# Turning from layer 0 to layer 1 in a two-layer encoder step: order of ScalarE and Pool, two more PSUM banks for the output sums, three early value tiles

## The chip, the cores and the metric

The kernel runs on one core of one Trainium2 chip. The metric is device time in microseconds of one execution, start to end. Of the core's engines the text names PE (TensorE, the matmuls), ACT (ScalarE), DVE (VectorE), POOL (GpSimd) and SP (SyncE, which issues most transfers). Every engine works through its own list of instructions in order; an instruction that waits holds up all behind it on that engine.

## The reference

One step of a two-layer encoder for 512 prompt rows and 64 sample rows of width 1024, in float32. Each layer normalises, projects, mixes in two attention branches, projects out, normalises again and adds. What matters for the change is the seam between the layers: layer 0's `rmsnorm(mp, norm_post)` and sum, layer 1's `rmsnorm(xp, norm_pre)`, and the first q, k and v of layer 1's band attention.

```python
def rmsnorm(x, g):
    y = x * lax.rsqrt(jnp.mean(x * x, axis=-1, keepdims=True) + EPS)
    return y * g

for l in range(DEPTH):
    hp, hs = rmsnorm(xp, norm_pre[l]), rmsnorm(xs, norm_pre[l])
    if l % 2 == 0:
        mp, stp = even_mixer(hp, pos_p, None, *w)
        ms, sts = even_mixer(hs, pos_s, caches, *w)
    else:
        mp, stp = odd_mixer(hp, pos_p, None, *w)
        ms, sts = odd_mixer(hs, pos_s, caches, *w)
    xp = xp + rmsnorm(mp, norm_post[l])
    xs = xs + rmsnorm(ms, norm_post[l])

# in odd_mixer: q_c, k_c, v_c, ... = split_cols(h @ w_in, ODD_SIZES)
# return mixed @ w_out, states
```

## The kernel before

The 512 prompt rows are four tiles of 128, called t0 to t3; the 64 sample rows are a fifth tile, NT (the number 4). Float32 products are made of three matmuls on a high and a low part of each factor: ACT casts the high part (L173 for weights, L224 for activations), and POOL (L177, weights) or DVE (L225, activations) subtracts to get the low part. PSUM has eight banks, dealt out in rings: psA 2, psS 2, psT 2, psU 1, psX 1 (L119).

**The end of layer 0** is `out_second` (L718). For each tile, in the order NT, t0 to t3, it makes four sums of 256 columns (c = 0 to 3, 12 matmuls each for a prompt tile, L270), in a bank of psA. DVE adds the bank to the partial result `m` (L745). After every second sum ACT squares the half row (L747) with the sum of squares read out behind it, into the bank of psX. After the fourth, POOL makes the root in two steps, `rstd_of2` (L197, L198); `m` is multiplied by the norm's weights (L751, on POOL for NT, t0, t1, on DVE for t2 and t3), and DVE multiplies by the root and adds the residual (L754). Then `sink0` (L1200) writes the row out, takes the next norm, `put_h` (L205: two squares on ACT L211, root on POOL, product on DVE L214), and `put_hT` (L217) transposes the result in eight 128x128 transposes on PE (L221) into psT; ACT copies the high part (L224), DVE makes the low part (L225). `out_second` runs again at the end of layer 1, with a sink that only writes the rows out (L1398).

**The start of layer 1** clears some tiles on POOL (L1221, L330, L334, L335), prepares bias tiles there (L1232, L1233, L1271) and starts the first pair of band heads, `qk_pair` (L337). Its q and k are made in two cuts of the rows (L35): the first takes rows 0 to 255 (t0, t1; 24 + 24 matmuls of 256 columns, L260), the second rows 256 to 575 (t2, t3, NT; 24 + 24 matmuls of 320 columns). `q_cb` empties a q bank (ACT L347, DVE L348, once for each of the two heads), `k_cb` a k bank (ACT L364 twice and L365, POOL L371, a transfer). Between the cuts, `early_v` makes value tiles t0 and t1 (24 matmuls each, L270, then a copy on ACT L407, a split on DVE, a transfer out). Behind the second cut and the transposes of k (L382, L384) come value tiles t2, t3 and NT (L278 is the sample's).

The order of each engine's list is not written by hand: a scheduler orders all instructions when the program is built, by its own estimate of when each would be ready, within the dependences and the priorities in the text (`tc.high_priority`). So an edit that moves one instruction can move others. `tc.issue_after(x)` keeps the instructions inside it behind x where both are on the same engine; it adds no wait between engines.

## Time and profile before

| | |
|---|---|
| time, median of 3 runs (lowest, highest) | 835.13 us (834.76, 836.82) |
| the profiled execution's own time | 829.8 us |
| its span, first to last instruction | 827.9 us |
| granted PE clock, mean | 0.984 of full speed |
| busy: PE, DVE, ACT, POOL | 93%, 61%, 60%, 46% of the span |
| the turn, layer 0's last sums to layer 1's sample value tile | about 380 to 455 us |

All times in the text are microseconds from the start of the profiled span. In a timeline row the first number is the start, the second the length, then engine, line, operation, output<-input, shape and count, and in brackets how long the engine was idle before and whose end released it. A matmul's length is that of the pipeline; the next starts before it ends, so the pace is read from the starts.

### The profile page before, as it was taken

What the parts mean: (1) busy time and instruction counts of PE and PEld (TensorE: products, weight loads), DVE (VectorE), ACT (ScalarE), POOL (GpSimd) and SP (SyncE); (2) the same over time, 40 slices, a digit from 0 to 9 for tenths busy, and PEclk for the clock granted to TensorE, in tenths of its full rate; (3) what the DMA queues carried; (4) which work ended last, traced back from release to release, by engine and by line L of the source; (5) the groups of instructions that cost most, each with busy time, mean ns of one, the idle gap of its engine ahead of it and who ended that gap; (6) DMA issues with size and microseconds to landing.
All of it is one profiled execution on the core that took longest, in us unless ns stands there. A gap on an engine that the chain in (4) does not pass through costs nothing.

```text
span 827.9 us, 16285 instructions
## 1 busy us (share of the span) xinstructions
PE 766.3 (93%) x5581; PEld 713.1 (86%) x5581; DVE 507.6 (61%) x1318; ACT 499.2 (60%) x1342; POOL 382.6 (46%) x461
## 2 busy tenths in 40 slices
PE   6989999999997999989868999999997999999986
PEld 4989899989895888788767999999897899998986
DVE  4544765777847675738962654664754576658345
ACT  7554664776747675666542755575644767768521
POOL 7584342654427131055772644553344444546453
PEclk9999999999999999999998999999999999999999
DMA  8243324441123022146352443433223543551562
GB/s 271 60 145 114 101 73 146 142 122 53 54 68 109 29 73 74 40 139 218 122 171 72 123 118 104 136 110 99 87 81 111 170 127 111 158 140 55 158 228 102
DMA packets 69924, 95.52 MB, mean 115 GB/s; under 512 B 9529, under 2 KB 40489, under 8 KB 69810
## 3 DMA queue, kind: packets, MB, share of 16 engines
q1 hardware_dynamic: 69264, 94.12, 37.7%
q8 instruction: 44, 0.72, 0.4%
q14 instruction: 38, 0.31, 0.2%
q10 hardware_dynamic: 578, 0.37, 0.1%
HBM read 74.36 MB, written 18.79 MB: 113 GB/s over the span
## 4 chain that ended last, share of the span: by engine, by line
PE 70%; DVE 10%; ACT 7%; DMA 5%; issue 4%; POOL 4%; SPq 1%; DVEq 0%; POOLq 0%; ACTq 0%
PE psA L260 27%; PE psA L270 15%; PE psU L435 5%; PE psX L528 4%; PE psT L426 4%; PE psA L278 3%; PE psS L563 2%; PE psS L460 2%; PE psS L461 2%; POOL m L751 1%; DMA part<-part 1%; PE psT L509 1%; ACT whi L173 1%; DMA x<-in_x_prompt_dram 1%; PE psA L989 1%
## 5 line engine op out<-in xcount | busy, mean ns | idle before, releaser
L260 PE MATMUL psA<-hT,whi 128*128 128x320 f32 (+1 forms) x1216 | 258.5, 301 | 3.8 <-DVE foxqbl L353 2.0
L177 POOL TENSOR_TENSOR wlo<-wraw,whi 128x512 fp32r<-128x512 f32 (+2 forms) x130 | 168.6, 1307 | 188.4 <-ACT whi L173 146.2
L260 PEld LDWEIGHTS psA<-hT,whi 128*128 128x128 f32 x1216 | 198.8, 190 | 6.8 <-issue 2.7
L260 PE MATMUL psA<-hT,wlo 128*128 128x320 f32 (+1 forms) x608 | 183.5, 302 | 0.0
L270 PE MATMUL psA<-whi,hT 128*128 128x256 f32 (+2 forms) x812 | 162.8, 287 | 6.8 <-DVE m L745 5.5
L270 PEld LDWEIGHTS psA<-whi,hT 128*128 128x128 f32 x812 | 130.0, 188 | 9.5 <-DVE m L745 6.4
L270 PE MATMUL psA<-wlo,hT 128*128 128x256 f32 (+2 forms) x420 | 121.2, 288 | 0.0
L260 PEld LDWEIGHTS psA<-hT,wlo 128*128 128x128 f32 x608 | 115.8, 190 | 0.8
L173 ACT CAST whi<-wraw 128x512 fp32r<-128x512 f32 (+2 forms) x130 | 78.2, 616 | 39.8 <-PE psA L260 21.4
L270 PEld LDWEIGHTS psA<-wlo,hT 128*128 128x128 f32 x420 | 79.5, 189 | 0.8
L371 POOL TENSOR_TENSOR kz<-kf,r 64x256 fp32r<-64x256 f32 x48 | 36.7, 765 | 30.5 <-ACT kf L365 28.8
L430 DVE TENSOR_TENSOR pt1l<-psT,pt1h 128x384 fp32r<-128x384 f32 x64 | 39.6, 620 | 14.6 <-ACT pt1h L429 13.7
L1237 DVE CUSTOM_DVE_ANT_0 x<-psS,T 128x128 f32<-128x128 f32 (+1 forms) x64 | 31.0, 484 | 23.0 <-PE psT L426 8.5
L447 POOL TENSOR_TENSOR g<-g,oT 128x512 f32<-128x512 f32 x14 | 18.3, 1304 | 53.8 <-DVE oT L439 53.5
L541 POOL TENSOR_TENSOR sK<-kraw,sK 128x384 fp32r<-128x384 f32 (+2 forms) x32 | 30.3, 946 | 26.3 <-ACT sK L540 24.6
L469 ACT ACTIVATE psS<-x,st 128x128 f32<-128x128 f32 (+1 forms) x64 | 34.1, 532 | 13.8 <-DVE st L1237 13.5
L429 ACT CAST pt1h<-psT 128x384 fp32r<-128x384 f32 x64 | 33.9, 531 | 12.6 <-PE psT L426 11.7
L528 PE MATMUL psX<-vs,sP 128*128 128x256 f32 (+1 forms) x184 | 38.6, 303 | 1.5 <-DVE sP L515 1.2
L439 DVE SCALAR_TENSOR_TENSOR oT<-psU,oT 64x256 f32<-64x256 f32 x64 | 26.8, 419 | 18.6 <-ACT oT L438 17.7
L460 PE MATMUL psS<-r,r 128*128 128x256 f32 (+1 forms) x96 | 35.4, 370 | 2.6 <-DVE st L1237 1.7
L347 ACT ACTIVATE r<-psA 64x256 fp32r<-64x256 f32 x48 | 18.2, 378 | 32.4 <-PE psA L260 16.9
L472 DVE TENSOR_SCALAR x<-psS,st 128x128 f32<-128x128 f32 (+1 forms) x64 | 35.1, 548 | 1.3
(390 smaller groups left out, 1893.9 us busy)
## 6 DMA issues: line engine op xcount, KB each, us to landing
wraw<-in_ws_dram SPq DMA_DIRECT2D x80, 256.0 KB
wraw<-in_w_out_dram SPq DMA_DIRECT2D x32, 256.0 KB
x<-in_x_prompt_dram SPq DMA_DIRECT2D x16, 256.0 KB
part<-part SPq DMA_DIRECT2D x32, 128.0 KB
m<-part SPq DMA_DIRECT2D x16, 256.0 KB
r<-r SPq DMA_DIRECT2D x48, 64.0 KB
out_dram<-kout SPq DMA_DIRECT2D x12, 256.0 KB
out_dram<-vf SPq DMA_DIRECT2D x24, 128.0 KB
```

The source lines that it names most:

```text
L173: nc.scalar.copy(hi, raw)
L177: eng.tensor_sub(lo, raw, f32(hi))
L260: nc.tensor.matmul(ps[:, :c1 - c0], w[:, k % 4, :], h.m[k // 4][:, k % 4, x, c0:c1], start=(k == 0 and n == 0), stop=(k == KT - 1 and n == 2))
L270: nc.tensor.matmul(ps[:, :n], h.m[k // 4][:, k % 4, x, t * P:(t + 1) * P], w[:, k % kp, :], start=(k == ks[0] and m == 0), stop=(k == ks[- ...
L371: nc.gpsimd.tensor_sub(pair.kl[s][me, cs], kf[me, cs], f32(k[me, cs]))
L429: nc.scalar.copy(ph[:, :i + 1, at], tv)
L430: nc.vector.tensor_sub(pl[:, :i + 1, at], tv, f32(ph[:, :i + 1, at]))
L435: nc.tensor.matmul(po, m.v[p // 2, j][:, p % 2, s * P:(s + 1) * P], x[:, j, :], start=(j == 0 and x is ph), stop=(j == 2 * hq + 1 and x is ...
L460: nc.tensor.matmul(ps[:, :w], pair.qq[s][:, q], pair.kk[s][:, :w], start=True, stop=False)
L469: nc.scalar.activation(ps[:, :n], src, AF.Exp, bias=mn, scale=-1.0, accum_out=sm)
L472: nc.vector.tensor_scalar(out=w[:, :n], in0=ps[:, :n], scalar1=rs, scalar2=None, op0=ALU.mult)
L528: nc.tensor.matmul(po[:, :256], l, r, start=(first and n == 0), stop=(last and n == len(ops) - 1))
```

## The change

Four edits. (1) The ACT instructions that empty the banks of the first cut (`q_cb`, `k_cb`) are kept behind the last square of layer 0's `out_second`. (2) The clearing and bias work on POOL is kept behind the last root, that of t3's `put_h`. (3) In `out_second` the odd sums (c = 1, 3) of t1 to t3 go to the banks of psS instead of psA, in both layers. (4) `early_v` makes three value tiles, t0, t1 and t2.

```diff
--- before.py
+++ after.py
@@ -1,4 +1,4 @@
-from contextlib import ExitStack
+from contextlib import ExitStack, nullcontext
 
 import numpy as np
 
@@ -195,8 +195,10 @@
 
         v, r = St([P, 1]), St([P, 1])
         RS.tensor_scalar(out=v[:rows], in0=ss[:rows, :1], scalar1=ss[:rows, 1:], scalar2=EPS, op0=ALU.add, op1=ALU.add)
-        nc.gpsimd.tensor_tensor(out=r[:rows], in0=v[:rows], in1=mhalf[:rows], op=ALU.pow)
+        roots.append(nc.gpsimd.tensor_tensor(out=r[:rows], in0=v[:rows], in1=mhalf[:rows], op=ALU.pow))
         return r
+
+    roots = []
 
     RS = nc.gpsimd if RSP else nc.vector
     ROOT = 1.0 / 32
@@ -334,13 +336,24 @@
         nc.gpsimd.memset(f32(m.qbh), 0.0)
         nc.gpsimd.memset(f32(m.qbl), 0.0)
 
-    def qk_pair(m, p, wq, wk, qs, h, kdst, ksdst, rooms=(), between=None):
+    def qk_pair(m, p, wq, wk, qs, h, kdst, ksdst, rooms=(), between=None, behind=None):
 
         pair = Mech()
         pair.qq = [Rr([P, S]), Rr([P, S])]
         sides = [(slice(64 * s, 64 * s + 64), slice(64 - 64 * s, 128 - 64 * s)) for s in range(2)]
 
+        def queued(c0):
+            return tc.issue_after(behind.ins) if behind and not c0 else nullcontext()
+
         def q_cb(ps, c0, c1):
+            with queued(c0):
+                q_bank(ps, c0, c1)
+
+        def k_cb(ps, c0, c1):
+            with queued(c0):
+                k_bank(ps, c0, c1)
+
+        def q_bank(ps, c0, c1):
             cs = slice(c0, c0 + 256)
             for s, (me, ot) in enumerate(sides):
                 q = pair.qq[s]
@@ -358,7 +371,7 @@
 
         pair.kl = m.kz[p % 2]
 
-        def k_cb(ps, c0, c1):
+        def k_bank(ps, c0, c1):
             cs = slice(c0, c0 + 256)
             for s, (me, ot) in enumerate(sides):
                 nc.scalar.copy(pair.kk[s][me, cs], ps[me, :256])
@@ -713,6 +726,8 @@
             wc.append(ws)
         return wc
 
+    squares = []
+
     def out_second(wc, f, half, part, tags, npost, xsrc, sink):
 
         ks = range(4 * half, 4 * half + 4)
@@ -736,7 +751,8 @@
                 for c in range(4):
                     m = ms[t][c // 2]
                     cs = slice(c % 2 * 256, (c % 2 + 1) * 256)
-                    ps = psA()
+
+                    ps = psS() if c % 2 and 0 < t < NT else psA()
                     if t == NT:
                         tm_sample(ps, 256, wc[c], f, ks)
                         nc.vector.tensor_add(m[:DS, cs], ps[DS:P, :256], m[:DS, cs])
@@ -744,8 +760,8 @@
                         tm_prompt(ps, 256, wc[c], f, ks, t)
                     nc.vector.tensor_add(m[:rows, cs], ps[:rows, :256], m[:rows, cs])
                     if c % 2:
-                        nc.scalar.activation(psX()[:rows], m[:rows], AF.Square, scale=ROOT,
-                                             accum_out=ss[:rows, c // 2:c // 2 + 1])
+                        squares.append(nc.scalar.activation(psX()[:rows], m[:rows], AF.Square, scale=ROOT,
+                                                            accum_out=ss[:rows, c // 2:c // 2 + 1]))
                         if c == 3:
                             r = rstd_of2(ss, rows)
                         (nc.vector if t in VT else nc.gpsimd).tensor_mul(
@@ -1218,7 +1234,10 @@
     lf = l1.tile([P, NT + 1, H], F32, name="lf")
     band.kz = fox.kz = [[l1.tile([P, S], F32R, name=nm("kz")) for s in range(2)] for i in range(2)]
     npost = l1.tile([P, D], F32, name="npost1")
-    nc.gpsimd.memset(lf, 0.0)
+
+    last_norm = roots[-1].ins
+    with tc.issue_after(last_norm):
+        nc.gpsimd.memset(lf, 0.0)
     st_t = open_pool(T=3, sx=4, kraw=1, vraw=1, sK=2, sP=2, vs=1, sat=2)
 
     rel = a["relb"]
@@ -1229,8 +1248,9 @@
     def band_bias(h):
         T = ring([P, S], F32, "T")
         rel_rows(T, h, 0, S)
-        nc.gpsimd.tensor_scalar(out=T, in0=T, scalar1=-1.0, scalar2=0.0, op0=ALU.mult, op1=ALU.add)
-        nc.gpsimd.memset(T[0:64, 0:64], BIG)
+        with tc.issue_after(last_norm):
+            nc.gpsimd.tensor_scalar(out=T, in0=T, scalar1=-1.0, scalar2=0.0, op0=ALU.mult, op1=ALU.add)
+            nc.gpsimd.memset(T[0:64, 0:64], BIG)
         return T
 
     def biased(ps, n, b, x, mn):
@@ -1268,23 +1288,26 @@
             T = ring([P, S], F32, "T")
             for s in range(2):
                 rel_rows(T[64 * s:64 * s + 64], 2 * p + s, 64 + TT - k0 - w, w)
-            nc.gpsimd.tensor_scalar(out=T[:, :w], in0=T[:, :w], scalar1=-1.0, scalar2=0.0, op0=ALU.mult, op1=ALU.add)
+            with tc.issue_after(last_norm):
+                nc.gpsimd.tensor_scalar(out=T[:, :w], in0=T[:, :w], scalar1=-1.0, scalar2=0.0, op0=ALU.mult,
+                                        op1=ALU.add)
             biased(ps[:, :w], w, T[:, :w][:, ::-1], x[:, :w], mn)
         po, rs = yield from s_soft(p, chunks_of(CL), score,
                         lambda c: s_vals(a["band_v"][p], c, band.vn[:, p * P:(p + 1) * P]), s_new)
         s_gate(s_fold(po, rs), gates[p])
 
     nc.sync.dma_start(npost, bcast(a["norm_post"][1:2, :], D))
-    clear(band)
-    clear_keys(band.kz)
+    with tc.issue_after(last_norm):
+        clear(band)
+        clear_keys(band.kz)
     wv = []
 
     def early_v():
         wv[:] = tm_weights(a["w_vc"][0])
-        v_chunk(band, 0, wv, h1, o["p_bandv"], (0, 1))
-
-    pr = band_qk(0, [bp.tile([P, 512], F32R, name=nm("w0"), tag=f"g{i}", bufs=1) for i in range(8)], early_v)
-    v_chunk(band, 0, wv, h1, o["p_bandv"], (2, 3, NT))
+        v_chunk(band, 0, wv, h1, o["p_bandv"], (0, 1, 2))
+
+    pr = band_qk(0, [bp.tile([P, 512], F32R, name=nm("w0"), tag=f"g{i}", bufs=1) for i in range(8)], early_v, squares[-1])
+    v_chunk(band, 0, wv, h1, o["p_bandv"], (3, NT))
     for p in range(NPAIR):
         nxt = band_qk(p + 1) if p < 3 else None
         if p == 1:
@@ -1399,7 +1422,8 @@
 
     part1 = dp.tile([TT, D], F32, name="part1")
     mix1 = new_feat(big1)
-    clear(fox)
+    with tc.issue_after(last_norm):
+        clear(fox)
     pr = fox_qk(0)
     for p in range(NPAIR):
         nxt = fox_qk(p + 1) if p < 3 else None
```

The number and kind of instructions is the same; their order differs at the turn and in the last output stage. In the rows that follow the numbers behind names tell tiles apart; line numbers of the changed program are higher by 2 to 20.

PE around the transposes of t3 (psT_5895 and psT_5902). psA_6077, psA_6108 and, in the changed program, psA_6139 are early value tiles (t0, t1, t2). Before, and then changed:

```order
L270 MATMUL psA_6108<-whi_6072,hT_5395 128x256 x2
L221 MATMUL psT_5806<-ident,x_5424 128x128 x4
L270 MATMUL psA_6108<-wlo_6073,hT_5395 128x256
L270 MATMUL psA_6108<-whi_6072,hT_5395 128x256
L221 MATMUL psT_5895<-ident,x_5431 128x128 x4
L221 MATMUL psT_5902<-ident,x_5432 128x128 x4
L260 MATMUL psA_6139<-hT_5393,w_1314_5963 128x320
L260 MATMUL psA_6172<-hT_5393,w_1318_5967 128x320
```

```order
L262 MATMUL psA_6021<-hT_5395,w_1320_5969 128x256 x2
L262 MATMUL psA_6021<-hT_5395,w_1321_5970 128x256
L223 MATMUL psT_5895<-ident,x_5431 128x128 x4
L223 MATMUL psT_5902<-ident,x_5432 128x128 x4
L272 MATMUL psA_6077<-whi_6054,hT_5393 128x256
L272 MATMUL psA_6077<-wlo_6055,hT_5393 128x256
L272 MATMUL psA_6077<-whi_6054,hT_5393 128x256 x2
```

Before, value tiles t0 and t1 stand ahead of t3's transposes, and the second cut (psA_6139) right behind them. Now the first cut's last matmuls (psA_6021) stand ahead of them, and the value tiles behind.

POOL around the root of t1's output norm (st_5683, st_5684); st_5697 and st_5698 are the root of t1's next norm, the wlo tiles weight splits for the value tiles. Before, and then changed:

```order
L751 TENSOR_TENSOR m_5413<-m_5413,npost 128x512
L197 TENSOR_SCALAR st_5683<-ss_5621 128x1
L751 TENSOR_TENSOR m_5414<-m_5414,npost 128x512
L198 TENSOR_TENSOR st_5684<-st_5683,mhalf 128x1
L197 TENSOR_SCALAR st_5697<-st_5692 128x1
L198 TENSOR_TENSOR st_5698<-st_5697,mhalf 128x1
L177 TENSOR_TENSOR wlo_6055<-wraw_6053,whi_6054 128x512
```

```order
L767 TENSOR_TENSOR m_5413<-m_5413,npost 128x512
L177 TENSOR_TENSOR wlo_6055<-wraw_6053,whi_6054 128x512
L197 TENSOR_SCALAR st_5683<-ss_5621 128x1
L767 TENSOR_TENSOR m_5414<-m_5414,npost 128x512
L177 TENSOR_TENSOR wlo_6061<-wraw_6059,whi_6060 128x512
L177 TENSOR_TENSOR wlo_6067<-wraw_6065,whi_6066 128x512
L198 TENSOR_TENSOR st_5684<-st_5683,mhalf 128x1
L177 TENSOR_TENSOR wlo_6073<-wraw_6071,whi_6072 128x512
L177 TENSOR_TENSOR wlo_6306<-wraw_6304,whi_6305 128x512
L197 TENSOR_SCALAR st_5697<-st_5692 128x1
L198 TENSOR_TENSOR st_5698<-st_5697,mhalf 128x1
```

One weight split now stands ahead of the root and two between its halves; two more stand ahead of the next root. The clearing (L1221, now L1240) moves from a few rows behind these to behind t3's last root.

ACT around t3's squares (m_5429 and m_5430; L747, now L763). r_5971 and r_5972 are the first cut's q, psT_5703 and psT_5710 the transposes of t1. Before, and then changed:

```order
L211 ACTIVATE psX_5789,st_5788<-m_5421 128x512
L211 ACTIVATE psX_5791,st_5788<-m_5422 128x512
L347 ACTIVATE r_5971<-psA_5992 64x256
L347 ACTIVATE r_5972<-psA_5992 64x256
L364 CAST r_5974<-psA_6021 64x256
L364 CAST r_5975<-psA_6021 64x256
L747 ACTIVATE psX_5842,ss_5813<-m_5429 128x512
L365 COPY kf_5973<-psA_6021 128x256
L747 ACTIVATE psX_5873,ss_5813<-m_5430 128x512
```

```order
L226 CAST hT_5393<-psT_5703 128x4x128
L226 CAST hT_5395<-psT_5710 128x4x128
L213 ACTIVATE psX_5789,st_5788<-m_5421 128x512
L213 ACTIVATE psX_5791,st_5788<-m_5422 128x512
L763 ACTIVATE psX_5842,ss_5813<-m_5429 128x512
L763 ACTIVATE psX_5873,ss_5813<-m_5430 128x512
L213 ACTIVATE psX_5885,st_5884<-m_5429 128x512
L213 ACTIVATE psX_5887,st_5884<-m_5430 128x512
L226 CAST hT_5393<-psT_5799 128x4x128
L226 CAST hT_5395<-psT_5806 128x4x128
L360 ACTIVATE r_5971<-psA_5992 64x256
L226 CAST hT_5393<-psT_5895 128x4x128
```

The copies of the first cut stood ahead of t3's squares (L347, L364) or between them (L365) and now stand behind both, and t3's norm squares (psX_5885, psX_5887) and t2's copies stand ahead of them too.

On PE the sums also change places: 54 matmuls of the psS sums of t1 and t2 (psS_5636, psS_5667, psS_5732, psS_5763) and of t1's first sum (psA_5622) stand ahead of the end of t0's fourth sum (psA_5571), which had none of them ahead of it.

## Rows read from the trace of the kernel before

**Rows 1.** The page's first part: busy us, share of the span, instructions of each engine.

```profile
PE 766.3 (93%) x5581; PEld 713.1 (86%) x5581; DVE 507.6 (61%) x1318; ACT 499.2 (60%) x1342; POOL 382.6 (46%) x461
```

**Rows 2.** Timeline of PE, 388 to 456 us: start, length, line, operation, [idle before, releaser].

```profile
390.26 0.28 PE L435 MATMUL psU<-pt1h,v 128*128 128x256 f32 x1
...
397.37 0.39 PE L270 MATMUL psA<-whi,hT 128*128 128x256 f32 x1 [1.10 <-DVE m L745]
...
401.26 0.38 PE L270 MATMUL psA<-whi,hT 128*128 128x256 f32 x1 [0.79 <-DVE m L745]
...
435.95 1.94 PE L221 MATMUL psT<-ident,x 128*128 128x128 f32 x8 [5.74 <-DVE x L214]
437.71 8.33 PE L260 MATMUL psA<-hT,w 128*128 128x320 f32 x48
...
449.21 0.38 PE L270 MATMUL psA<-whi,hT 128*128 128x256 f32 x1 [0.45 <-ACT kout L384]
...
455.00 0.28 PE L278 MATMUL psA<-whi,hsT 128*128 128x256 f32 x1
```

**Rows 3.** Timeline of PE, 470 to 490 us: 24 matmuls of 320 columns, and a wait.

```profile
477.33 0.44 PE L382 MATMUL psA<-ident,kf 128*128 128x128 f32 x2 [0.62 <-ACT kf L365]
...
481.49 0.45 PE L260 MATMUL psA<-hT,whi 128*128 128x320 f32 x2
...
485.09 0.40 PE L563 MATMUL psS<-sK,bandqbh 128*128 128x256 f32 x2
```

**Rows 4.** Timeline of DVE (VectorE), 408 to 456 us.

```profile
409.79 3.47 DVE L214 SCALAR_TENSOR_TENSOR x<-m,st,npre 128x512 f32<-128x512 f32 x2
...
419.13 0.41 DVE L745 TENSOR_TENSOR m<-psA,m 128x256 f32<-128x256 f32 x1
...
435.06 1.42 DVE L214 SCALAR_TENSOR_TENSOR x<-m,st,npre 128x512 f32<-128x512 f32 x2 [0.84 <-POOL st L198]
```

**Rows 5.** Timeline of ACT (ScalarE), 408 to 456 us.

```profile
421.73 0.38 ACT L347 ACTIVATE r<-psA 64x256 fp32r<-64x256 f32 x1 [0.48 <-DVE r L348]
...
424.36 0.59 ACT L747 ACTIVATE psX<-m 128x512 f32<-128x512 f32 x1
...
425.46 0.61 ACT L747 ACTIVATE psX<-m 128x512 f32<-128x512 f32 x1
425.99 0.19 ACT L747 ACTIVATION_READ_ACCUMULATOR psX<-m 128x1 f32 x1
...
431.63 0.60 ACT L211 ACTIVATE psX<-m 128x512 f32<-128x512 f32 x1 [1.70 <-DVE m L754]
...
437.07 0.59 ACT L224 CAST hT<-psT 128x512 fp32r<-128x512 f32 x1 [3.35 <-PE psT L221]
437.93 0.59 ACT L224 CAST hT<-psT 128x512 fp32r<-128x512 f32 x1 [0.27 <-PE psT L221]
```

**Rows 6.** Timeline of POOL, 400 to 433 us.

```profile
402.18 1.30 POOL L751 TENSOR_TENSOR m<-m,npost 128x512 f32<-128x512 f32 x1
...
409.72 2.99 POOL L177 TENSOR_TENSOR wlo<-wraw,whi 128x512 fp32r<-128x512 f32 x2
...
429.65 0.44 POOL L197 TENSOR_SCALAR st<-ss 128x1 f32<-128x1 f32 x1
```

**Rows 7.** Engines by stretch: busy us (instructions), granted clock, DMA share, GB/s.

```profile
376.00:386.00 10.00, 9.25 (x70) 8.20 (x69) 9.74 (x25) 6.80 (x19) 3.83 (x4) 1.00 0.80 270
...
430.00:440.00 10.00, 4.26 (x18) 3.64 (x18) 6.46 (x11) 4.07 (x10) 2.51 (x5) 0.66 0.26 92
```

**Rows 8.** Timeline of the last output stage, PE and DVE.

```profile
791.11 0.39 PE L278 MATMUL psA<-whi,hsT 128*128 128x256 f32 x1 [1.64 <-ACT part L698]
...
802.69 0.39 PE L270 MATMUL psA<-whi,hT 128*128 128x256 f32 x1 [1.12 <-DVE m L745]
...
823.64 1.41 DVE L754 SCALAR_TENSOR_TENSOR m<-m,st,x 128x512 f32<-128x512 f32 x2 [0.84 <-POOL st L198]
```

## The prediction

> **What bounds the kernel now.** I read the page's busy times first: PE is busy for 93% of the span [rows 1], so a change that adds no matmul can win only where PE waits, and loses where it makes PE wait. Next I read PE's timeline through the turn, the stretch in which layer 0's second output projection ends and layer 1 begins. The reader is to see two kinds of wait [rows 2]. Four are short, 0.8 to 1.1 us and 3.8 us together (the longest and the shortest stand there): the next output sum waits for VectorE to empty a bank (L745). One is long: 5.74 us before the last prompt tile's (t3's) eight transposes, which start at 435.95. From there the chain is fixed: transposes, the second cut of q and k (48 matmuls from 437.71), a short bank wait, value tiles t2 and t3 from 449.21, and the sample value tile at 455.00. I call 455.00 the turn's end; it lies 19.05 us behind t3's transposes. After it PE is filled: up to 520 us its one marked wait is 0.62 us [rows 3], so a later turn's end is a later kernel's end, nearly one for one.
>
> Then I read the two queues that t3's norm stands in. ScalarE: the last sum is added at 419.13 for 0.41 us [rows 4], but t3's first square starts only at 424.36 and the second at 425.46 [rows 5]; 4.8 us lie in between, behind the first cut's copies. Pool: the second square's sum is read out at 426.18, and Pool starts the root's first half at 429.65 [rows 6], 3.5 us late. So 8.3 us of queue stand ahead of 435.95. That is what edits 1 and 2 aim at. The prediction rests on what else the new order does.
>
> **The change, part by part.** Durations are from the profiled execution (829.8 us, span 827.9), which lies 5.3 us below the median of the runs; I work out a difference and add it to the median, 835.13.
>
> *Value tiles (edit 4).* Before, value tiles t0 and t1 stand ahead of t3's transposes and fill PE while t3's norm runs. In the new order all three early tiles stand behind t3's transposes. PE works its queue in order, so they cannot start while t3's norm is running: 5.8 us of work (two tiles, 48 matmuls of 0.12 us, as from 449.21 to 455.00 [rows 2]) leave the wait and come behind it.
>
> What then stands between t3's transposes and the turn's end: (i) the first value tile needs the bank of the first q cut, whose ScalarE copies now queue behind the last squares: t3's first copy done 1.7 us after the transposes begin, then a key split, the second q copy and VectorE's, 0.4 each (the q copy 0.38 [rows 5]), with hand-offs 3.1. (ii) Three value tiles, 72 matmuls of 0.12: 8.6, and 0.3 for a slow start. (iii) The second cut, 2 x 3.60 us at full clock (24 matmuls from 481.49 to 485.09 [rows 3]): 7.2. (iv) From its end to the next value tile before: 437.71 + 8.33 = 446.04 to 449.21, 3.2; the same steps, 3.0 taken. (v) Value tile t3: 2.9. Sum 25.1 us against 19.05. **At an unchanged start of t3's transposes the new order costs 6.05 us.** It gains only if they start before 429.9.
>
> *When t3's transposes start.* Edits 1 and 2 take the 8.3 us away, but edit 3 lets the sums of t1 to t3 run ahead, and t0 pays. PE now runs 54 matmuls (12 + 12 + 9 + 9 + 12) ahead of the end of t0's fourth sum, which ended at 390.26 before [rows 2]: 54 x 0.12 = 6.5, so 396.7. Its square stands behind the sample tile's transposes and copies; for t3 these take 435.95 to 438.52 [rows 2, 5], two thirds of it for the smaller tile: t0's second square at 398.4. From there the tiles go in rounds, since ScalarE's order is now norm squares of one tile, then output squares of the next. A round with no queue is 4.9 us: from second square to the next norm's first square 6.17 - 3.47 = 2.7 (425.46 to 431.63 less Pool's queue [rows 5, 6]), and three squares of 0.73. Added to it:
> - t1: 1.3 for a multiply (L751) between the root's halves on Pool [rows 6] and 0.6 for a weight split between the squares: 405.2.
> - t2: the root of t1 has a multiply and, new, weight splits around it, one ahead and two between its halves: 1.3 + 3 x 1.5 [rows 6]. VectorE's pair then runs beside more splits; such a pair took 3.47 beside them and 1.42 without [rows 4]: 2.0 more. 405.2 + 4.9 + 5.8 + 2.0 = 417.9.
> - t3: t1's two copies stand ahead of t2's norm squares, 1.2, and a multiply on VectorE 0.7: 424.7, before 425.46.
> - Transposes: 435.95 - 425.46 - 3.47 = 7.0, and 1.3 for two multiplies that hid in Pool's queue before: 433.0.
>
> Hand-offs of about 0.1 us at each of some twenty steps are partly in these terms; counted in full, 435.0, which I take. Bounds: 433.0 with none, 437.5 if the weight splits meet all of VectorE's pairs. So the promised 8.3 us are spent: t3's transposes start about where they did. Turn's end 435.0 + 25.1 = 460.1, **5.1 us later**; with the bounds 3.1 to 7.6.
>
> *Pool's clearing (edit 2)* is 6 to 7 us of memsets and bias work that now runs behind the last root, while PE works on the value tiles; nothing needs it before the second cut's copies, some 20 us on. Cost nothing; without that cover, 6 us. *The moved value tile's* copy, split and output transfer run beside matmuls: nothing.
>
> *The last output stage (edit 3 again).* The same bank rule applies in layer 1. The odd sums of t1 to t3 run early there too, so t0's and t1's even sums come late, and the final rows of t1, t2 and t3 are made one straight after another at the end. Six halves of 256 KB are 1.57 MB; at the 270 GB/s of the busiest stretch [rows 7] they need 5.8 us, about as long as VectorE takes to make them, so the last write waits for others where before it stood alone (last step 823.64 + 1.41 = 825.05 [rows 8], span's end 2.85 later). From below: PE's two waits there, 1.64 and 1.12 us [rows 8], could go, -2.8. From above: the backlog of two halves and a hand-off, +3.5. I take +1.5, since the end is set by the last tile's norm, which keeps its length, and only the write behind it is longer.
>
> Sum: 5.1 + 1.5 = 6.6 us; 835.1 + 6.6 = **841.7 us**, and 836.4 for a profiled execution like this one.
>
> **A rule against the rows.** By the rows, banks cost the sums 3.8 us in four short waits [rows 2], and none of them sets the end: t3's last sum is in at 419.5, 16 us ahead of its transposes. The Trainium skill (Perfetto Trace Analysis, section Matmuls) says that independent matmul groups should rotate through different PSUM banks so that emptying one overlaps the next; by it alone edit 3 would bring 3.8 us, and the sum would be 2.8.
>
> Behind the 5.74 us wait PE's granted clock is 0.66 over 430 to 440 us [rows 7], a mix of 1.2 and 2.4 GHz, and the second cut took 8.33 us instead of 7.2: a long wait costs 1.1 us on top. The new order has two such waits, about 8 us before t1's transposes and 4 before t3's. The Trainium skill (TensorE: Matmul & The Clock Gate, section What's actually happening) says that the throttled state is the default and activity releases it; the row agrees, and it speaks against an order that leaves PE without filler.
>
> **Rivals.**
> - *The queues vanish and nothing else is lost* (faster). t3's transposes start 8.3 us earlier, at 427.65; the turn's end is 427.65 + 25.1 = 452.75, 2.25 earlier: 832.9, and 830.1 if the last stage's waits go too. It decides at 429.9. For it: both queues are in the rows. Against it: the 54 matmuls ahead of t0 and Pool's splits ahead of t1's root are in the order itself. 0.07.
> - *The rounds run long* (slower still). The transposes start at 438 and the value tiles run at half clock at first, 1.1: turn's end 464.2, 9.2 later, last stage 3.0: 847.3. 0.07.
> - *No change.* The splits fall clear of t1's root, the transposes start near 430.5 and the last stage costs nothing: 835.7. That the order doesn't change is excluded: it is written in the order of both programs. 0.06.
> - Forecast: 0.80, between 838 and 846.
>
> About 0.3%, 2.5 us, can be told from no change. Faster takes the first rival, 0.07; same the third, 0.06; slower the forecast and the second, 0.87. The range, 838 to 848, leaves out the first and the third and the far end of the second, and holds the bounds of the turn and of the last stage.
>
> **What would show it.** Right: counted from the last instruction that both programs share ahead of the turn, t3's transposes start within 3 us of before, behind a wait on VectorE; the three value tiles follow them; Pool has weight splits around t1's root; PE waits some 8 us before t1's transposes; and the turn's end comes 24 to 26 us after t3's transposes instead of 19. Wrong: t3's transposes over 5 us earlier, or PE's waits at the turn shorter in sum than before.

## The result and the profile after

The changed kernel takes 842.55 us (median of four runs, 838.08 to 845.64), the kernel before beside it 835.41: a ratio of 1.0091 [1.0066, 1.0116], slower, and 7.1 us where 6.6 were forecast. The profiled execution is the quickest of the four, 838.08 us with a span of 836.2; before had 829.8 and 827.9, so the two traces differ by 8.3 us. I explain these 8.3. They are cut at four points that both programs share. The first is an attention score matmul ahead of the turn: in PE's timeline of before it is the row

```profile
375.97 0.48 PE L976 MATMUL psS<-kh,r 96*128 96x512 f32 x1
```

and of after the first row below. The lines used here are 2 to 16 higher in the changed program: L221 is L223, L260 L262, L270 L272, L278 L280, L745 L761, L747 L763, L751 L767, L754 L770. In the page's first part the counts of instructions are those of [rows 1] and the busy times nearly so; PE's is 2.6 us longer. The rest of the time is waiting.

```profile
PE 768.9 (92%) x5581; PEld 715.7 (86%) x5581; DVE 505.5 (60%) x1318; ACT 498.9 (60%) x1342; POOL 379.9 (45%) x461
```

PE's timeline of after through the turn, to be held against [rows 2]:

```profile
375.52 0.48 PE L992 MATMUL psS<-kh,r 96*128 96x512 f32 x1
...
409.80 1.04 PE L223 MATMUL psT<-ident,x 128*128 128x128 f32 x8
419.49 1.94 PE L223 MATMUL psT<-ident,x 128*128 128x128 f32 x8 [8.66 <-DVE x L216]
...
422.54 5.28 PE L262 MATMUL psA<-hT,w 128*128 128x256 f32 x32 [0.48 <-DVE hT L227]
...
433.04 1.97 PE L223 MATMUL psT<-ident,x 128*128 128x128 f32 x8 [2.71 <-DVE hT L227]
436.11 0.55 PE L272 MATMUL psA<-whi,hT 128*128 128x256 f32 x1 [1.10 <-DVE r L361]
...
446.06 7.20 PE L262 MATMUL psA<-hT,w 128*128 128x320 f32 x48
...
455.62 0.39 PE L272 MATMUL psA<-whi,hT 128*128 128x256 f32 x1 [0.49 <-ACT kout L397]
...
458.58 0.28 PE L280 MATMUL psA<-whi,hsT 128*128 128x256 f32 x1
```

The short bank waits of 1.10 and 0.79 in [rows 2] are gone from the output sums (what is left of them there is 0.22 and 0.17). The 5.74 before t3's transposes became 8.66 before t1's, with nothing on PE to fill it. From the first point to the sample value tile the turn lasts 83.06 us; before it was 455.00 - 375.97 = 79.03. That is **4.0 us**.

The last stage, against [rows 8]: PE, then DVE, then the chain of waits.

```profile
795.05 0.39 PE L280 MATMUL psA<-whi,hsT 128*128 128x256 f32 x1 [0.78 <-ACT part L711]
...
800.77 0.48 PE L272 MATMUL psS<-whi,hT 128*128 128x256 f32 x1 [3.45 <-DVE m L761]
```

```profile
800.29 0.42 DVE L761 TENSOR_TENSOR m<-psS,m 128x256 f32<-128x256 f32 x1 [3.55 <-DMA m<-part]
...
826.97 1.40 DVE L770 SCALAR_TENSOR_TENSOR m<-m,st,x 128x512 f32<-128x512 f32 x2
828.30 0.41 DVE L761 TENSOR_TENSOR m<-psA,m 128x256 f32<-128x256 f32 x1
...
831.89 1.42 DVE L770 SCALAR_TENSOR_TENSOR m<-m,st,x 128x512 f32<-128x512 f32 x2 [0.45 <-POOL st L198]
```

```profile
788.81 5.46 DMA part<-part
795.96 4.31 DMA m<-part
800.77 2.83 PE psS L272 x12
```

DVE adds t1's odd sum (a psS bank) early in this stage, and must wait until t1's partial result, stored earlier, is loaded back. All that stands behind it on DVE waits too, the emptying of the psA banks among it, and so does PE, whose next psS sum needs the bank that this add empties. The chain of before has no `m<-part` in it. From the sample's first sum to the end of the span the stage takes 836.2 - 795.05 = 41.15 us, before 827.9 - 791.11 = 36.79: **4.35 us**. The stretch between turn and last stage is longer by 0.36, and the first point is 0.45 earlier: 4.03 + 4.35 + 0.36 - 0.45 = 8.3.

### The profile page after: what moved, and what is told of

It is laid out like the page before. It is cut to its first block, busy times and chain, and to the rows that moved or that the text cites. A ratio compares the mean times of both kernels' runs of the same rounds, so it can differ in the third digit from the quotient of the medians.

```text
span 836.2 us, 16283 instructions
## 1 busy us (share of the span) xinstructions
PE 768.9 (92%) x5581; PEld 715.7 (86%) x5581; DVE 505.5 (60%) x1318; ACT 498.9 (60%) x1342; POOL 379.9 (45%) x461
## 3 DMA queue, kind: packets, MB, share of 16 engines
q1 hardware_dynamic: 69264, 94.12, 37.7%
## 5 line engine op out<-in xcount | busy, mean ns | idle before, releaser
L262 PE MATMUL psA<-hT,whi 128*128 128x320 f32 (+1 forms) x1216 | 256.3, 299 | 4.6 <-DVE foxqbl L366 2.0
L262 PEld LDWEIGHTS psA<-hT,whi 128*128 128x128 f32 x1216 | 196.6, 189 | 7.8 <-issue 2.7
L262 PE MATMUL psA<-hT,wlo 128*128 128x320 f32 (+1 forms) x608 | 182.3, 300 | 0.0
L272 PE MATMUL psA<-whi,hT 128*128 128x256 f32 (+2 forms) x764 | 154.0, 289 | 2.8 <-DVE r L361 1.1
L272 PEld LDWEIGHTS psA<-whi,hT 128*128 128x128 f32 x764 | 123.5, 190 | 4.7 <-issue 1.5
L272 PE MATMUL psA<-wlo,hT 128*128 128x256 f32 (+2 forms) x396 | 115.5, 292 | 0.0
L262 PEld LDWEIGHTS psA<-hT,wlo 128*128 128x128 f32 x608 | 114.6, 189 | 0.8
L272 PEld LDWEIGHTS psA<-wlo,hT 128*128 128x128 f32 x396 | 76.1, 192 | 0.8
L482 ACT ACTIVATE psS<-x,st 128x128 f32<-128x128 f32 (+1 forms) x64 | 34.1, 533 | 13.4 <-DVE st L1257 13.1
L451 ACT ACTIVATE oT<-psU 64x256 f32<-64x256 f32 x64 | 24.3, 379 | 19.2 <-PE psU L448 18.0
```

Of the source, the lines that this page charges most:

```text
L262: nc.tensor.matmul(ps[:, :c1 - c0], w[:, k % 4, :], h.m[k // 4][:, k % 4, x, c0:c1], start=(k == 0 and n == 0), stop=(k == KT - 1 and n == 2))
L272: nc.tensor.matmul(ps[:, :n], h.m[k // 4][:, k % 4, x, t * P:(t + 1) * P], w[:, k % kp, :], start=(k == ks[0] and m == 0), stop=(k == ks[- ...
L482: nc.scalar.activation(ps[:, :n], src, AF.Exp, bias=mn, scale=-1.0, accum_out=sm)
```

## The experiments

My theory was that edit 3 alone costs, through the order that it brings on engines that work their lists in turn: in layer 0 t0's norm comes late, in the last stage DVE waits for a load; and that edits 1, 2 and 4 gain. The rivals: the loss is in the value tiles behind t3's transposes (the 6.05 us of the prediction), or in ScalarE's and Pool's moved work, or in the banks themselves. In the expectations A is the theory I held before that run, B its rival. Diffs are against the changed kernel unless said. Ratios are to the kernel before on the same chip. The turn is counted as above; "rest" is from its end to the span's end, and "last stage" is the part of it from the sample's first sum on.

| run | kept of the change | median us | ratio | turn | rest | last stage |
|---|---|---|---|---|---|---|
| before | nothing | 835.41 | 1 | 79.03 | 372.90 | 36.79 |
| after | 1, 2, 3, 4 | 842.55 | 1.0091 [1.0066, 1.0116] | 83.06 | 377.62 | 41.15 |
| e1 | 1, 2, 4 | 827.69 | 0.9937 [0.9915, 0.9960] | 75.26 | 373.50 | 36.73 |
| e2 | 1, 2, 4, and 3 in layer 0 | 836.93 | 1.0045 [1.0024, 1.0066] | 83.00 | 375.49 | 37.74 |
| e3 | 3 in layer 1 | 838.95 | 1.0061 [1.0040, 1.0082] | 79.18 | 377.61 | 41.66 |
| e4 | 1, 2, 3 | 841.54 | 1.0108 [1.0081, 1.0134] | 84.49 | 378.76 | 41.65 |
| e5 | 1, 2 | 830.69 | 0.9977 [0.9959, 0.9995] | 77.72 | 374.47 | 37.67 |
| e6 | all, value tiles put ahead | 846.89 | 1.0172 [1.0141, 1.0203] | 85.68 | 379.37 | 41.68 |
| e7 | 1, 2, 4, and 3 in layer 1, held | 827.09 | 0.9928 [0.9908, 0.9949] | 73.39 | 371.77 | 36.43 |
| e8 | 1, 2, 4, and 3 in layer 0, held | 831.72 | 0.9987 [0.9964, 1.0010] | 78.36 | 373.07 | 36.85 |
| e9 | all, both layers held | 836.31 | 1.0009 [0.9989, 1.0028] | 84.04 | 373.36 | 36.36 |
| e10 | 1 | 831.80 | 0.9960 [0.9944, 0.9976] | 78.94 | 373.10 | 36.80 |
| e11 | 2 | 830.09 | 0.9934 [0.9909, 0.9959] | 76.01 | 372.98 | 36.71 |
| e12 | 4 | 831.82 | 0.9954 [0.9939, 0.9970] | 77.79 | 374.71 | 36.72 |

Turn, rest and last stage come from one profile each. e1 and e7, whose edits differ in the last stage alone, have turns 1.9 us apart; I read nothing into a turn that differs by less. The last stage is steadier: 36.4 to 37.7 us in the ten kernels without the wait for the load, 41.2 to 41.7 in the four with edit 3 free in layer 1. The runs were made in three sets, and the kernel before, beside them, had medians of 833.57 (e1 to e4), 833.24 (e5 to e8) and 836.00 us (e9 to e12). It moved by 0.33% from one set to another, so a difference of that size between runs of two sets shows nothing.

### Edit 3 taken out, and put in one layer at a time

e1:

```diff
-                    ps = psS() if c % 2 and 0 < t < NT else psA()
+                    ps = psA()
```

> The change without its third edit: all sums of the output stage stay in psA; the queueing of ScalarE and Pool and the three early value tiles stay. Theory A (the two more banks let the scheduler run later tiles' sums ahead of t0's, and that order is the whole loss): the value tiles stand ahead of t3's transposes again, the 8.3 us of queue are gone, the turn's end comes 4 to 8 us before that of the kernel before, the last stage is as before; 827 to 832 us. Theory B (the queued copies hold the first cut's banks and a third value tile stands in the way; the banks are harmless): 838 to 843 us.

e2:

```diff
+        first = not squares
...
-                    ps = psS() if c % 2 and 0 < t < NT else psA()
+                    ps = psS() if first and c % 2 and 0 < t < NT else psA()
```

> The change with the psS banks in layer 0's output stage only. Theory A: the turn as in the changed kernel, 3.9 us late, and the last stage as before, without PE's wait of 3.45 us for t1's odd sum; 838 to 839.5 us. Theory B (the last stage's 4.4 us are a later consequence of the turn, not of its own banks): 842 to 843 us.

e3, the kernel before with:

```diff
-                    ps = psA()
+                    ps = psS() if not first and c % 2 and 0 < t < NT else psA()
```

> The kernel before with one thing added: the psS banks in layer 1's output stage. Theory A: turn as before, last stage 4.4 us longer with a wait of PE on a sum that waits for a partial result's transfer; 839 to 840 us. Theory B: 835 us, no such wait.

e1 is 0.63% faster than before where the whole change is 0.91% slower: edit 3 is the loss, and without it the other three gain. The turn is 3.8 us shorter, a little under the 4 to 8 of theory A. PE's timeline of e1:

```profile
421.08 4.39 PE L262 MATMUL psA<-hT,w 128*128 128x256 f32 x35 [2.23 <-DVE hT L227]
...
428.16 0.39 PE L272 MATMUL psA<-whi,hT 128*128 128x256 f32 x1 [1.82 <-ACT kf L378]
...
435.58 0.60 PE L223 MATMUL psT<-ident,x 128*128 128x128 f32 x4
```

Two value tiles stand ahead of t3's transposes again, at 428.16, and the transposes, as late as in [rows 2], wait for nothing. In e2 the turn is as long as with the whole change, in e3 the last stage is. PE's timeline of e2, then of e3, then DVE's of e3:

```profile
420.30 1.94 PE L223 MATMUL psT<-ident,x 128*128 128x128 f32 x8 [8.65 <-DVE x L216]
```

```profile
797.32 0.39 PE L272 MATMUL psS<-whi,hT 128*128 128x256 f32 x1 [3.92 <-DVE m L762]
```

```profile
796.84 0.42 DVE L762 TENSOR_TENSOR m<-psS,m 128x256 f32<-128x256 f32 x1 [4.02 <-DMA m<-part]
```

e2 shows the 8.65 us wait and no wait for the load; e3 shows the load, and its turn is that of before. The two losses are separate, and each is edit 3's. The time of e2, 836.93, lies below both of its ranges; of the 2.6 us by which its rest exceeds that of before, 1.0 lie in the last stage.

### The value tiles' place

e4, two early tiles instead of three, and e5, the same without edit 3:

```diff
-        v_chunk(band, 0, wv, h1, o["p_bandv"], (0, 1, 2))
+        v_chunk(band, 0, wv, h1, o["p_bandv"], (0, 1))
...
-    v_chunk(band, 0, wv, h1, o["p_bandv"], (3, NT))
+    v_chunk(band, 0, wv, h1, o["p_bandv"], (2, 3, NT))
```

> The change with two early value tiles instead of three. Theory A: the third tile is work that PE does either ahead of the second cut or behind it, both behind t3's transposes; no change against the changed kernel, 841 to 843 us. Theory B (the third tile is in the way of the second cut): 2.9 us less, 839 to 840 us.

> The kernel before with the first two edits alone (ScalarE's copies behind the last square, Pool's clearing behind the last root); two early value tiles, psA only. Theory A (the 8.3 us of queue ahead of t3's transposes are real and the two value tiles stay ahead of these): the transposes start at once behind the value tiles, the turn's end comes 4 to 6 us earlier; 828 to 830 us. Theory B (the queues only moved: without a third tile PE waits again for t3's norm): 832 to 834 us.

e6, t3's transposes held behind the three value tiles:

```diff
-        put_hT(h, rows, t * P, h1)
+        if t == 3:
+            late.append((h, rows, t * P, h1))
+        else:
+            put_hT(h, rows, t * P, h1)
...
-        v_chunk(band, 0, wv, h1, o["p_bandv"], (0, 1, 2))
+        last = v_chunk(band, 0, wv, h1, o["p_bandv"], (0, 1, 2))
+        with tc.issue_after(last.ins):
+            put_hT(*late[0])
```

> The changed kernel with one thing forced: t3's transposes stand behind the three early value tiles on PE. The 54 matmuls ahead of t0's fourth sum and the last stage stay as in the change. Theory A (the value tiles' place is worth about 6 us of the turn): the turn's end 4 to 6 us earlier than in the changed kernel, about that of the kernel before or 2 us ahead; 836 to 838 us. Theory B (the late start of t0's norm is the whole loss, the tiles' place follows from it and costs nothing): 841 to 843 us.

e4 is as slow as the whole change; whether two or three tiles are early is not what costs. e5 lies between its theories: t3's transposes start at 433.75 without a wait, as A has it, but the turn is only 1.3 us shorter than before, not 4 to 6; its last two prompt value tiles take 7.3 us (447.0 to 454.3) instead of 5.8, at a granted clock of 0.77. e6 is slower still than the change, where A had 836 to 838 and B 841 to 843: **my theory that the tiles lose by standing behind the transposes fell.** Its PE, ACT and DVE timelines:

```profile
439.25 0.55 PE L272 MATMUL psA<-whi,hT 128*128 128x256 f32 x1 [5.14 <-DVE r L363]
```

```profile
434.01 0.38 ACT L362 ACTIVATE r<-psA 64x256 fp32r<-64x256 f32 x1
437.84 0.40 ACT L555 CAST sK<-kraw 128x256 fp32r<-128x256 f32 x1 [3.44 <-DMA kraw<-in_band_kT_dram]
438.27 0.38 ACT L362 ACTIVATE r<-psA 64x256 fp32r<-64x256 f32 x1
```

```profile
438.68 0.43 DVE L363 SCALAR_TENSOR_TENSOR r<-psA,r 64x256 fp32r<-64x256 f32 x1 [1.38 <-ACT r L362]
```

The first value tile needs the bank of the first q cut, and by edit 1 that bank is emptied behind the last squares, which come late. Ahead of the transposes the tile only waits for it, and with it the transposes. 3.44 of the 5.14 us are a wait of ACT for a key load (in the changed kernel the cast of the same keys, at 434.68, waits for none), so the price of the place alone is not measured. But 846.9 less 3.4 is still no gain on 842.6. I conclude, without a run that shows it alone, that in the changed kernel the tiles' place follows from the late squares and is no cost of its own beside them.

### The banks with the old order

e7 is e1 with the psS banks in layer 1, each sum there held behind the one before it; e8 is the change with the psS banks in layer 0 only, each odd sum held (`prev` is the last matmul of the sum before, `after(x)` is `tc.issue_after(x.ins)`; in e7 it holds in layer 1 alone, in e8 in both layers, and both hold the sample's sums as well):

```diff
-                    ps = psS() if c % 2 and 0 < t < NT else psA()
+                    ps = psS() if not first and c % 2 and 0 < t < NT else psA()
...
-                        tm_prompt(ps, 256, wc[c], f, ks, t)
+                        with after(prev):
+                            prev = tm_prompt(ps, 256, wc[c], f, ks, t)
```

```diff
-                    ps = psS() if c % 2 and 0 < t < NT else psA()
+                    ps = psS() if first and c % 2 and 0 < t < NT else psA()
...
-                        tm_prompt(ps, 256, wc[c], f, ks, t)
+                        with after(prev if c % 2 else None):
+                            prev = tm_prompt(ps, 256, wc[c], f, ks, t)
```

> The kernel of e1 plus the psS banks in the last stage, with its sums kept in the order of the kernel before (each sum's matmuls behind the sum before). Theory A (the last stage loses by its order, a sum that waits for a partial result ahead of all others, and not by its banks): no wait of 3.5 us; as e1 or up to 1.5 us less, PE's two short waits for a bank: 826 to 828 us. Theory B (the banks themselves cost): 831 to 833 us.

> The change with psS banks in layer 0 only, each odd sum held behind the sum before it on PE. Theory A: t0's fourth sum keeps its place, the value tiles come ahead of t3's transposes; the banks then pay what PE's four short waits cost at most: 825 to 828 us, against 836.9 without the hold. Theory B (an order that is not the old one costs, held or not): 833 to 837 us.

e9, all four edits, sums and transposes of both layers held in the old order:

```diff
-                        tm_prompt(ps, 256, wc[c], f, ks, t)
+                        with after(prev, hts.get(order[order.index(t) - 2]) if c == 3 and t in (1, 2, 3) else None):
+                            prev = tm_prompt(ps, 256, wc[c], f, ks, t)
```

> All four edits, psS banks in both layers, but the sums of both output stages held on PE in the order of the kernel before, with the transposes of each tile between them as before. Theory A (the order is the loss, not the banks): the turn as in e1 or up to 3 us shorter, the last stage as in e7; 824 to 829 us. Theory B (odd sums in psS cost by themselves, held or not, as e8's 831.7 could be read): 831 to 834 us.

e7 settles the last stage: with the same banks and the old order the wait for the load is gone, and it is the fastest version of all, equal to e1 within the intervals. PE's timeline of its last stage has the two waits of [rows 8] and no third like 3.45:

```profile
784.97 0.39 PE L281 MATMUL psA<-whi,hsT 128*128 128x256 f32 x1 [1.14 <-ACT part L713]
...
796.54 0.39 PE L272 MATMUL psA<-whi,hT 128*128 128x256 f32 x1 [1.15 <-DVE m L768]
```

So there the order cost, not the banks; and the banks by themselves gave nothing. For layer 0 the answer is half: holding the odd sums took 4.6 of e2's 83.00 us away, but the turn stays 3.1 above e1's, between A and B. PE's timeline of e8, at t0's transposes, then DVE's and ACT's ahead of them:

```profile
408.70 0.80 PE L223 MATMUL psT<-ident,x 128*128 128x128 f32 x4 [2.35 <-DVE x L216]
410.38 1.09 PE L223 MATMUL psT<-ident,x 128*128 128x128 f32 x4 [0.88 <-DVE x L216]
```

```profile
388.30 0.67 DVE L955 TENSOR_REDUCE st<-psS 128x1 f32<-128x512 f32 x1
```

```profile
389.00 0.66 ACT L484 ACTIVATE psS<-psS,st 128x512 f32<-128x512 f32 x1 [0.79 <-DVE st L955]
```

The hold on PE also changed the lists of the other engines. PE starts the last scores of layer 0 at 384.38, 6.0 us from the first point, and in e1 at 6.8 (383.22). But DVE's reduction for the last softmax now stands behind other work, so this softmax starts at 10.6 us from the first point, in e1 at 8.9 (385.31). So 1.8 us of delay come from ahead of the output norms; how much of the 3.1 they make is not shown.

e9 was to close this and did not: its 836.31 misses both ranges. Its profile is the slowest of its twelve runs, 839.92 (they go from 829.46). There layer 0's last attention work runs later still: on ACT's timeline a weight cast waits 3.77 us for its load and holds up the softmax of the next row; in e1 that softmax (379.74) stands ahead of the cast (381.24). The last softmax starts 13.1 us from the first point, 4.2 later than in e1:

```profile
385.99 0.62 ACT L173 CAST w<-wraw 128x512 fp32r<-128x512 f32 x1 [3.77 <-DMA wraw<-in_ws_dram]
386.51 0.66 ACT L485 ACTIVATE psS<-psS,st 128x512 f32<-128x512 f32 x1
...
393.70 0.66 ACT L485 ACTIVATE psS<-psS,st 128x512 f32<-128x512 f32 x1 [0.79 <-DVE st L963]
```

Its last stage, 36.36, is that of a kernel without the load wait, as in e7; its turn cannot be compared. Whether the two banks would pay in layer 0 in exactly the old order stays open.

### Edits 1, 2 and 4 each alone

e10 passes `squares[-1]` to `band_qk` and undoes the rest; e11 keeps the `tc.issue_after(last_norm)` blocks alone; e12 the three early tiles alone. In short, against the changed kernel (all three also with `ps = psA()`):

```diff
-    with tc.issue_after(last_norm):
+    with nullcontext():
```

```diff
-    pr = band_qk(0, [...], early_v, squares[-1])
+    pr = band_qk(0, [...], early_v)
```

The first of these pieces is in e10 and e12, the second in e11 and e12; e10 and e11 have e4's two early tiles.

> The kernel before with the first edit alone. Theory A (the queues add up and Pool's 3.5 us stays; the order now also has t3's transposes ahead of 16 value matmuls): the turn within 1 us of before, 832 to 835 us. Theory B (ScalarE's queue is the longer and decides): the turn 3 to 5 us shorter, 828 to 830 us.

> The kernel before with the second edit alone. Theory A (Pool's queue came last before t3's root, so taking it away shows at once): t3's transposes 3 to 3.5 us earlier, the turn 2 to 3 us shorter, 830 to 832 us. Theory B (the clearing itself comes late for the first keys): 833 to 835 us.

> The kernel before with the fourth edit alone. Theory A (a third value tile ahead of t3's transposes fills half of PE's 5.7 us wait): the turn 2 to 3 us shorter, 830 to 832 us. Theory B (the third tile holds a bank of the second cut, or its copy and split delay t3's norm): 833 to 836 us.

By the medians each gains 0.4 to 0.7%, all three together (e1) 0.6%, edits 1 and 2 together (e5) 0.2%. These come from three sets, so whether the gains add is not shown. e10's lies 0.2 below A's range, and its turn is as A has it; e11 and e12 are within A's ranges. The clearest is Pool's clearing: e11's turn is 3.0 us shorter. e12's is 1.2 shorter, less than a turn can be told by. Edit 1 alone leaves the turn as it was. Its second square of t3 is read out by 422.85 (before: 426.18), but Pool, with the clearing and bias work still in its list, starts the root at 429.27, 6.4 us late instead of 3.5. The rest comes back as waits for Pool's root of t2 and for the late bank, on PE's timeline of e10:

```profile
428.19 1.29 PE L223 MATMUL psT<-ident,x 128*128 128x128 f32 x8 [2.90 <-DVE x L216]
...
431.80 0.58 PE L272 MATMUL psA<-whi,hT 128*128 128x256 f32 x1 [2.33 <-ACT kf L378]
```

In e11 the bank wait is 0.37 us. So e10's gain is one of the medians alone: its profiled execution, 831.31 us, is longer than that of before, 829.8, which lies some 5 us below the median of before. Why the median is lower although the turn is not shorter I can't explain.

## Why the prediction was right, and which step was not

The sum was 6.6 us, the medians say 7.1 and the traces 8.3. It came out right partly because two errors met: the turn cost 1.1 less than taken, the last stage 2.9 more.

- **t0 pays 54 matmuls: right.** Its second square was put at 398.4. The ACT timeline of after, to be read with 0.45 added for the earlier first point:

```profile
397.70 0.61 ACT L763 ACTIVATE psX<-m 128x512 f32<-128x512 f32 x1
...
405.57 0.60 ACT L763 ACTIVATE psX<-m 128x512 f32<-128x512 f32 x1
...
418.31 0.60 ACT L763 ACTIVATE psX<-m 128x512 f32<-128x512 f32 x1
...
424.80 0.60 ACT L763 ACTIVATE psX<-m 128x512 f32<-128x512 f32 x1
```

- **The rounds: right.** Forecast 405.2, 417.9, 424.7; the rows are at 406.0, 418.8, 425.3 with the shift. The long step, t1 to t2, was 12.7 forecast and 12.74 measured. Its cause is in the POOL and DVE timelines of after: the splits stand where the order put them, and the VectorE pair beside them takes 3.43 us, like the 3.47 of [rows 4], not 1.42.

```profile
406.43 1.75 POOL L177 TENSOR_TENSOR wlo<-wraw,whi 128x512 fp32r<-128x512 f32 x1
408.27 0.62 POOL L197 TENSOR_SCALAR st<-ss 128x1 f32<-128x1 f32 x1
408.97 1.30 POOL L767 TENSOR_TENSOR m<-m,npost 128x512 f32<-128x512 f32 x1
410.21 2.51 POOL L177 TENSOR_TENSOR wlo<-wraw,whi 128x512 fp32r<-128x512 f32 x2
412.66 0.58 POOL L198 TENSOR_TENSOR st<-st,mhalf 128x1 f32<-128x1 f32 x1
```

```profile
405.25 3.47 DVE L216 SCALAR_TENSOR_TENSOR x<-m,st,npre 128x512 f32<-128x512 f32 x2 [0.28 <-POOL st L198]
...
413.27 3.43 DVE L770 SCALAR_TENSOR_TENSOR m<-m,st,x 128x512 f32<-128x512 f32 x2 [0.93 <-POOL st L198]
```

- **t3's transposes: the term was too long.** 435.0 was taken; they start at 433.04, 433.5 with the shift, near the lower bound of 433.0. From t3's second square it is 8.2 us, as the rows gave (433.0 - 424.7 = 8.3). The 2.0 added for hand-offs were mostly in the rows already. The last step was not the one I had: t3's norm product was done by 432.4, and the transposes waited for a bank of psT that DVE empties of t2's transposes. So the match of the length is in part luck. DVE's timeline of after:

```profile
432.30 1.28 DVE L227 TENSOR_TENSOR hT<-psT,hT 128x512 fp32r<-128x512 f32 x2
```

- **From the transposes to the turn's end: 25.1 forecast, 25.54 measured.** Bank wait and first tile 3.07 (3.1), three tiles 9.95 (8.9), second cut 7.20 (7.2), to the next tile 2.36 (3.0), tile t3 2.96 (2.9). Only the slow start was undersized: 1.3 us instead of 0.3, since the first thirteen matmuls came at half clock. The prediction itself prices a long wait at 1.1 us, but only its second rival charges that.
- **"At an unchanged start the new order costs 6.05": right as a sum (25.54 less 19.05 is 6.49), wrong as a reason.** I read the tiles' place as a cost by itself, to be earned back by an earlier start. e6 put the tiles ahead and gained nothing, and e1, with edit 4 kept, has two tiles ahead of the transposes and a shorter turn. What costs in the turn is that edit 3 makes t0's norm late (e2 against e1).
- **The last stage: the step that failed.** I wrote that the end is set by the last tile's norm, which keeps its length, and that only the write behind it is longer. The write is not longer: from the last DVE step (833.31) to the span's end it is 2.9 us, before 2.85. The norm itself comes later. Matmuls from the sample's first sum to the last sum's last take 31.5 us instead of 29.4. The 3.45 wait, sixteen matmuls at half clock behind it and a wait of 0.96 ahead of the last sum lengthen them; the 1.12 of [rows 8] is gone, and twelve matmuls, t1's early odd sum, now stand ahead of the stretch. Then the last sum stands on DVE behind another tile's norm (826.97), and its own norm takes 0.8 longer. I looked at banks and writes there, and not at what DVE's earliest sum must load. The bound of +3.5 was passed by 0.85.
- **Pool's clearing and the moved copies cost nothing: right;** e11 even gains, and e4, whose third tile stays in its old place, is no faster than the change.
- **The rule on banks.** The short waits did go from the sums, 1.10 and 0.79 to 0.22 and 0.17, and e1 against after prices edit 3 at 0.9937 to 1.0091, some 13 us (11.0 by the two spans). The Trainium skill (Perfetto Trace Analysis, section Matmuls) asks for rotation through different PSUM banks so that emptying overlaps the next group; here that overlap came and the time went up, by what the order did elsewhere.
- **The rule on the clock.** After's two waits were 8.66 and 2.71 us, forecast about 8 and 4. Both brought the low clock. The granted clock was 0.50 in the transposes and the first value matmuls behind the 2.71, and 0.71 in the 32 matmuls of the first cut behind the 8.66, which took 5.28 us where e1's 35 took 4.39 at 1.00. The windows of after:

```profile
433.00:435.00 2.00, 1.96 (x8) 1.56 (x8) 1.19 (x3) 0.81 (x2) 1.91 (x6) 0.50 0.47 131
436.10:439.00 2.90, 2.89 (x13) 2.90 (x14) 1.10 (x2) 1.34 (x4) 2.73 (x5) 0.50 0.36 89
...
422.50:427.60 5.10, 5.06 (x32) 5.06 (x33) 3.81 (x7) 2.37 (x8) 2.03 (x4) 0.71 0.33 124
```

The mechanism that I gave for the turn is thus shown by e1, e2 and e8 together with these rows, with 3.1 us of e8's turn left open; that of the last stage, which I had not forecast, by e3 and e7.

## What to carry to other kernels

A spare bank, or any edit that lets one engine run ahead, changes what stands ahead of what on every engine that works its list in order: ask which instruction now comes earlier than its data, and what is queued behind it. In a stage that reads back stored partial results, list for each first use when its load can have landed, as carefully as the banks. When several edits go in together, time each alone, beside the kernel before: here three of four gained, one of them by its median only, and the fourth turned the whole into a loss, and the version without it, or with its banks only where the order is held, beats both kernels (827.69 and 827.09 us).

## What the hardware did that I had not expected

The same wait did not always lower the clock. Ahead of the first cut, e1 and e11 have the same wait on PE, 2.23 us on the same line, and the same 35 matmuls behind it. In e1 they take 4.39 us, in e11 5.87:

```profile
423.37 5.87 PE L262 MATMUL psA<-hT,w 128*128 128x256 f32 x35 [2.23 <-DVE hT L227]
```

The windows of the two stretches, e1 and then e11 (clock, DMA share and GB/s are the last three numbers):

```profile
421.00:425.50 4.50, 4.42 (x37) 4.42 (x38) 3.48 (x8) 1.95 (x7) 2.02 (x4) 1.00 0.74 233
```

```profile
423.30:429.00 5.70, 5.63 (x35) 5.63 (x36) 4.62 (x10) 2.32 (x8) 1.93 (x4) 0.70 0.78 236
```

The granted clock was 1.00 in one and 0.70, a mix of 2.4 and 1.2 GHz, in the other. In e11 it did not fall in the wait: it was 1.00 over the first 0.7 us of work behind it and 0.50 from 424.7 to 427.5. A shorter wait can come with the low clock too: e1's first value tile starts behind 1.82 us of idling, and its granted clock was 1.00 up to 429.5 and 0.50 from 429.6 to 432.7. So in these traces a wait of about 2 us costs either its own length or up to 1.5 us more (5.87 - 4.39), and they don't tell which in advance.
